# Moving the statistics sums of a convolution branch out of the accumulators' PSUM, with one-bank tiles at the seam between two layers

## The chip, the core and the metric

The kernel runs on one core of a Trainium2 chip, as one program. Its time is the device time of one execution in microseconds (us). The engines are PE (TensorE, matrix products, with PEld for its weight loads), DVE (VectorE), ACT (ScalarE), POOL (GpSimd) and SP (SyncE, which here only issues DMAs). Each engine runs its own list of instructions in order and waits on semaphores for the others.

## The reference

One inference step of a trunk of two layers on 640 tokens (128 of a prompt, 512 of a sample), width 1024, all in float32:

```python
# layer 0, the convolution branch (h: the normalised and modulated input)
u = h @ w_in + b_in                        # 1024 -> 3 x 2048
a, a_gate, z = split(u, 3)
v = a * sigmoid(a_gate)
v = depthwise_conv(v, w_dw, b_dw)          # 31 taps; the sample's in rows of 64 tokens
v = silu(layer_norm(v, ln_g, ln_b))        # over the 2048 channels
x = x + gate * ((v * silu(z)) @ w_out)     # 2048 -> 1024
# layer 1, a bidirectional state-space branch on modulate(rms_norm(x))
z, xbc, dt = split(h @ w_in, ...)
xbc = silu(depthwise_conv(xbc, 5 taps))
y = ssd_scan(forward) + flip(ssd_scan(backward)) + d * xs
x = x + gate * (rms_norm_by_group(y * silu(z)) @ w_out)
return rms_norm(x)                         # and the prompt's final states
```

The layer norm needs, for each token, the sum of v and of v squared over the 2048 channels. These are the statistics sums of this document.

## The kernel before

**Tiling.** Channels lie on the 128 partitions, tokens on the free axis: an activation is a tile of 128 x 640, used as two halves of 320. Each float32 product is three products in a faster format: a weight is split into a high part `wh` and a low part `wl`, an input into `h_hi` and `h_lo`, and PE adds `h_hi·wh`, `h_lo·wh` and `h_hi·wl`. Layer 0 has 48 tiles of `w_in` (16 each of a, g, the gate, and z); one is 48 matmuls of 128x320 (L499) into a PSUM tile `u` of two banks out of a ring of two (`mm`), with tokens in columns 0 to 319 of each bank; columns 480 on are used for blocks of the modulation (L519, L128).

**Weights.** SP loads `wf`, ACT casts it to `wh` (L472). `wl` is made in one of two ways in `split`: DVE or POOL subtracts `wh` from `wf` (L477), or ACT writes −`wh` (L482) and a DMA issued by POOL adds the weight from memory onto it (L483). The first tile of layer 0 and those of layer 1 take the first way, all others the second.

**Convolution.** v = a·sigmoid(g) is written on DVE (L539). For each of 16 tiles ACT starts an accumulator in PSUM (L640), DVE adds its taps there (L648), ACT forms some taps (`tp`, L678) that POOL adds into an SBUF tile `cv` (L719), POOL also does the edges of the prompt (`seam`, L703, L707), and at the end both are summed: by ACT's copy (L655) and POOL's adds, for the last two tiles by DVE (L668). Two PSUM tiles of 128 x 1024, `cva`, are the accumulators of the even and of the odd tiles (columns 0 to 639); their columns 640 to 799 hold the statistics sums, `ssum`. ACT squares `cv`, and PE adds `cv` and its square there with a matrix of ones, 8 matmuls of 160 columns for a tile, recorded as 16 (L195, `quarter_sums`), accumulating over all 16 tiles. So a sum and the taps of the next tiles write the same PSUM tile, and PE and DVE take turns there. After the sixteenth sum come mean and variance (L727 to L737), the normalisation, the product with silu(z), and the product with `w_out`: `out_pass` for the output tiles 0 to 5, `out_halves` for 6 and 7, which are done by halves of tokens (L853).

**Seam.** Here layer 0's last output tiles, the root mean square for layer 1 (`root`: sums L899, its reciprocal, and its spread over the partitions L919), the modulation (`modo`, L936, then `h_hi` on ACT and `h_lo`, L945, on DVE) and the first three tiles of layer 1 (`dt` and two `xs`, L874) follow each other. The output tiles are `o__5673` (6) and `o__5675` (7), two banks each, a half in each bank; the spread is written into `o__5673` too, and the `dt` product into `o__5675`.

**Order.** What each engine does when is decided while the program is built. Pieces of work are generators ("chains") that yield operations, keys they need and ring slots they take; a planner, `Order`, puts the operations of all chains in a row on each engine by estimated times and by priorities (`PRIO0`, and `PRIO` in layer 1), and that order is kept. The order of PE's tiles is written out (`PLAN0` and `PLAN`); `NPOOL` says how many taps of each convolution tile go to POOL.

Of the kernel before, what the change touches and what calls it, by code (L numbers as in the profile page):

```python
# [40 lines left out]
PRIO0 = {"conv": 1, "after_a": -2, "after_g": 2, "init": -6, "late_taps": 3, "late_adds": -4, "seam": 6, "copied": 2, "after_z": -6, "weights": 3, "split": -2, "row": -6, "square": -2, "filler": 6, "blocks": 7, "add_sums": 1, "stats": 3, "means": -6, "normalise": -1, "gate_z": -1, "late_block": 4, "residual": 6, "half_residual": -2, "root": 3, "modulation": 1, "split_h": 0, "scales": 6}  # L41
PLAN0 = "a1 g2 g3 a2 g4 a3 g5 a4 g6 a5 a6 g7 g8 z0 a7 a8 g9 g10 a9 a10 g11 g12 a11 z1 a12 g13 a13 z2 z3 z4 g14 g15 a14 z5 a15 z6 z7 z8 z9 z10 z11 z12 z13 z14 z15"
NPOOL = (11, 8, 15, 11, 6, 10, 12, 5, 3, 9, 2, 2, 5, 8, 7, 6)
# [4 lines left out]
def trunk(ctx: ExitStack, tc: tile.TileContext, a: dict):  # L48
# [308 lines left out]
    pa_ctx = ExitStack()  # L357
# [55 lines left out]
    with tc.tile_pool(name="l0", bufs=1) as lp:  # L413
# [4 lines left out]
        mr = lp.tile([P, 2, QN], F32, name="mr")  # L418
# [16 lines left out]
        for name, n in (("wf", 2), ("wh", 1), ("wl", 1), ("mm", 0), ("tm", 2), ("v", 4), ("cv0", 1), ("cv1", 1), ("cva", 0), ("cs", 33), ("tp", 3), ("pr", 1), ("eb", 3), ("hT", 0)):  # L435
            run.ring(name, n, 1.0 if name == "cs" else -9.0)
# [19 lines left out]
        def split(name, wf, src):  # L456
# [12 lines left out]
            else:  # L469
# [6 lines left out]
                if name[0] == "l1" or name == ("w", tiles0[0]):  # L476
                    t = yield either((VL, 1.23, lambda: V.tensor_sub(out=wl, in0=wf, in1=wh.bitcast(F32))), (PO, 2.44, lambda: G.tensor_sub(out=wl, in0=wf, in1=wh.bitcast(F32))), bias=0.0)  # L477
                    put("wf", t)
                    post(name, t)
                    return  # L480
# [53 lines left out]
        def after_a(i, ps, n=None):  # L534
# [15 lines left out]
        def after_z(j, ps, n=None):  # L550
# [4 lines left out]
            if n is not None:  # L555
                yield from late_block(n, ps)
                t = max(t, run.keys["mod", n])
            put("mm", t)
# [16 lines left out]
        def square(j):  # L575
            yield key(("cv", j))
            yield get("tm")
# [4 lines left out]
            start(add_sums(j), t)  # L582

        begun = []

        def add_sums(j):
            def sums():
                begun.append(j)
                for t_, s in ((cv[j], 0), (sgs["sq", j], 1)):
                    quarter_sums(ssum[s], t_, len(begun) == 1, len(begun) == 16)  # L590
            t = yield op(PE, 0.78, sums)
            put("tm", t)
            post(("sums", j), t)

        def filler():
            for name in plan:
# [13 lines left out]
                elif name[0] == "z":  # L610
                    start(after_z(i, ps, n), t)
                else:
# [3 lines left out]
                    start(after_a(i, ps, n), t)  # L616
# [9 lines left out]
        accs, whole = {}, []  # L626
# [8 lines left out]
        def init():  # L635
            for i in range(16):
                yield key(("v", i))
                yield get(f"cv{i % 2}")
                accs[i] = whole[i % 2][:, 0:NT]
# [12 lines left out]
        def copied(i):  # L652
# [3 lines left out]
            put(f"cv{i % 2}", t)  # L656
# [9 lines left out]
        def last_add(i):  # L666
            yield key(("added", i))
            t = yield op(VE, 0.9, lambda: V.tensor_add(out=cv[i], in0=cv[i], in1=accs[i]))  # L668
            post(("cv", i), t)
# [53 lines left out]
        def stats():  # L723
            t = yield key(*[("sums", j) for j in range(16)])
            rq = mr[:, 1]
            start(means(), t)
            yield op(ACT, 0.35, lambda: S.activation(out=msq, in_=ssum[0], func=AF.Square, scale=1.0 / 2048))  # L727
            yield op(VE, 0.37, lambda: V.scalar_tensor_tensor(out=rq, in0=ssum[1], scalar=1.0 / 2048, in1=msq, op0=ALU.mult, op1=ALU.subtract))
            post(("read",), run.clock[VE])
# [6 lines left out]
        def means():  # L736
            t = yield op(VE, 0.33, lambda: V.tensor_scalar(out=mr[:, 0], in0=ssum[0], scalar1=1.0 / 2048, scalar2=None, op0=ALU.mult))  # L737
            t = max(t, (yield key(("read",))))
            put("cva", t)
            put("cva", t)  # L740
            yield from spread_row(0, mr[:, 0])
# [75 lines left out]
        def residual(m, ps, ring):  # L817
# [4 lines left out]
            put(ring, t)  # L822
            yield get("tm")
# [10 lines left out]
        def out_halves():  # L834
            po = []
            for m, ring in ((6, "cva"), (7, "mm")):
                yield get(ring)
                po.append(bank(ring, f"o{m}_"))
            last["o"] = po
            start(spare(), 0.0)  # L840
            for b, tok in enumerate((slice(0, HN), slice(HN, NT))):
                ks = [k for it in ((0, 1, 2, 3) if b == 0 else (0, 2, 3, 1)) for k in range(4 * it, 4 * it + 4)]
                every = [(j, k) for k in ks[:12] for j in range(2)] + [(j, k) for j in range(2) for k in ks[12:]]
                for j, k in every:
                    if b == 0:
                        yield key(("out", 2, k // 4))
                    w = W0["out", 2, k // 4]

                    def step():
                        o = (k % 4 * 2 + j) * 128  # L850
                        wh, wl = (w[0][:, o : o + 128], w[1][:, o : o + 128]) if len(w) == 2 else (w[n + o // 512][:, o % 512 : o % 512 + 128] for n in (0, 2))
                        for n, (w_, t_) in enumerate(((wh, yh[k]), (wl, yh[k]), (wh, yl[k]))):
                            T.matmul(po[j][:, b, 0:HN], lhsT=w_, rhs=t_[:, tok], start=k == ks[0] and n == 0, stop=k == ks[-1] and n == 2)  # L853
# [6 lines left out]
            first[:] = [last["o"][1], last["mm"], last["cva"]]  # L860
            for b, tok in enumerate((slice(0, HN), slice(HN, NT))):
                for k in range(KD):
                    yield key(("h", b, k))
                    for n in range(3):
                        if not k and not b:
                            yield key(("l1", n))
                        if not k and not n:
                            yield key(("half", b, 7), ("o",))
                        ps, (wh, wl), (hi, lo) = first[n], W0["l1", n], h1[k]

                        def step():
                            ws, wls = wh[:, k * 128 : k * 128 + 128], wl[:, k * 128 : k * 128 + 128]
                            for n_, (w, t_) in enumerate(((ws, hi), (ws, lo), (wls, hi))):
                                T.matmul(ps[:, b, 0:HN], lhsT=w, rhs=t_[:, tok], start=k == 0 and n_ == 0, stop=k == KD - 1 and n_ == 2)  # L874
# [4 lines left out]
        last = {}  # L879

        def spare():
            for ring in ("mm", "cva"):
                yield get(ring)
                last[ring] = bank(ring, "xs")
            post(("o",), 0.0)

        def half_residual(b, m, ps, tok):
            for cd, sl in SEGS:
                xv = x[m][:, tok][:, sl]
                t = yield op(VE, 0.26 + 0.2 * cd, lambda: V.scalar_tensor_tensor(out=xv, in0=ps[:, b, sl], scalar=gain(0, m, cd), in1=xv, op0=ALU.mult, op1=ALU.add))  # L890
            post(("half", b, m), t)
            yield get("tp")
            sq = last["sq", b, m] = lp.tile([P, 560], F32, tag="tp", bufs=3, name="rms_sq")
# [3 lines left out]
        def sums_x(b, n, t, tok):  # L897
            for q in (2 * b, 2 * b + 1):
                T.matmul(last["mm"][32 * q : 32 * q + 32, b, HN : HN + QN], lhsT=ones[:, 0:32], rhs=t[:, tok][:, q % 2 * QN : q % 2 * QN + QN], start=n == 0, stop=n == 2)  # L899

        def root(b):
            tok = slice(b * HN, b * HN + HN)
            rows = slice(64 * b, 64 * b + 64)
            yield key(("acc", 5), ("o",))
            t = yield op(PE, 0.2, lambda: sums_x(b, 0, racc[0], tok))
            if b:
                put("tm", t)
            for n in range(2):
                yield key(("half_sq", b, 6 + n))
                t = yield op(PE, 0.2, lambda: sums_x(b, 1 + n, last["sq", b, 6 + n], slice(0, HN)))  # L910
                put("tp", t)
            rq = mr[:, 0][rows]
            ps = last["o"][0]
            yield op(ACT, 0.42, lambda: S.activation(out=rq, in_=last["mm"][rows, b, HN : HN + QN], func=AF.Sqrt, scale=1.0 / 1024, bias=epsb[rows]), "sqrt")
# [1033 lines left out]
```

## Time and profile before

| | |
|---|---|
| time, median of 3 runs | 1105.62 us (1105.17 to 1105.71) |
| profiled execution | 1108.58 us, span of its instructions 1106.8 us |
| mean granted clock of PE | 0.988 |
| PE busy | 1061.7 us (96%) |
| DVE busy | 804.6 us (73%) |
| ACT busy | 650.8 us (59%) |
| POOL busy | 448.5 us (41%) |
| taps on DVE (L648) | 360, 277.7 us, mean 822 ns |
| statistics sums on PE (L195) | 256 records of matmuls, from 116.0 to 385 us |

The profile is one execution, recorded by the hardware; its times are us from the first instruction, and busy time is time in which an engine executes. The granted clock is the share of full speed at which PE was allowed to run. Layer 0 takes the span up to about 575 us, its convolution up to 385; layer 1 the rest. Lines such as L648 are lines of the kernel before; in the kernel after the same statements have other numbers (the taps are L686, the products L501).

### The profile page before, as it was taken

Reading aid. Unit: us, or ns where it says so; the run is one execution under the profiler, and the core shown is the slowest. Engines: PE = TensorE matmul, PEld = TensorE weight load, DVE = VectorE, ACT = ScalarE, POOL = GpSimd, SP = SyncE. Lnnn points to the kernel's source line nnn. Section 1 sums busy time; section 2 is a strip of 40 time slices with the busy share of each in tenths; the row PEclk is TensorE's granted clock in tenths of the full one; section 3 lists DMA queues with packets and bytes.
Section 4 is the critical chain, followed back from the end, with each engine's and each line's share of the span. In section 5 each row is a group of like instructions: output and inputs, shape, how many; then the busy total and the mean of one; then the engine's idle time right before and its main releaser. Section 6 shows DMA issues by size and latency. Waiting matters only on the chain. (4 is left out here: it accounts for less than half of the span.)

```text
span 1106.8 us, 19938 instructions
## 1 busy us (share of the span) xinstructions
PE 1061.7 (96%) x7904; PEld 979.2 (88%) x7904; DVE 804.6 (73%) x1181; ACT 650.8 (59%) x1070; POOL 448.5 (41%) x447
## 2 busy tenths in 40 slices
PE   6989999999999999999999999999999999999996
PEld 4879999989999999999799888898899888988886
DVE  2588898999997889102479778987776786687763
ACT  6556887866558678333367564793537563754442
POOL 2027999866349601111000056405551534362223
PEclk9989999999999999999899999999999999999998
DMA  9398777886866667667112463414343423433102
GB/s 364 150 260 216 177 186 161 202 198 147 207 139 136 145 135 152 149 149 163 58 40 77 117 146 105 115 57 110 95 109 90 124 86 87 134 86 105 40 20 95
DMA packets 86685, 147.46 MB, mean 133 GB/s; under 512 B 26944, under 2 KB 49856, under 8 KB 86592
## 3 DMA queue, kind: packets, MB, share of 16 engines
q1 hardware_dynamic: 77088, 113.91, 34.6%
q0 software_dynamic: 8784, 31.46, 17.0%
q8 instruction: 62, 1.02, 0.4%
q10 hardware_dynamic: 720, 0.82, 0.2%
q14 instruction: 31, 0.25, 0.1%
HBM read 141.25 MB, written 4.92 MB: 132 GB/s over the span
## 5 line engine op out<-in xcount | busy, mean ns | idle before, releaser
L648 DVE SCALAR_TENSOR_TENSOR cva<-v,cst,cva 128x610 f32<-128x610 f32 (+13 forms) x360 | 277.7, 822 | 26.3 <-PE cva L195 13.3
L719 POOL TENSOR_TENSOR cv<-cv,tp 128x490 f32<-128x490 f32 (+6 forms) x120 | 151.6, 1264 | 8.2
L472 ACT CAST wh<-wf 128x1024 fp32r<-128x1024 f32 x63 | 65.8, 1044 | 91.0 <-PE o__5231 L153 29.8
L1071 ACT CAST wh<-wf 128x1024 fp32r<-128x1024 f32 x53 | 55.5, 1048 | 87.1 <-PE o L1109 32.7
L678 ACT ACTIVATE tp<-v,cst 128x490 f32<-128x490 f32 (+6 forms) x120 | 83.0, 722 | 32.7 <-POOL cv L719 32.1
L1109 PE MATMUL o<-yhl,wh 128*128 128x320 f32 x384 | 94.0, 332 | 2.0 <-ACT zs L1228 1.9
L1075 DVE TENSOR_TENSOR wl<-wf,wh 128x1024 fp32r<-128x1024 f32 x49 | 65.0, 1326 | 31.0 <-ACT wh L1071 30.8
L1109 PE MATMUL pz<-h_hi,wh 128*128 128x320 f32 x256 | 85.5, 334 | 1.5 <-ACT up L1138 1.5
L1395 POOL TENSOR_TENSOR y<-y,yo 128x512 f32<-128x512 f32 x32 | 48.5, 1517 | 79.5 <-DVE yo L1393 79.5
L1109 PE MATMUL pz<-h_hi,wl 128*128 128x320 f32 x256 | 79.1, 309 | 0.0
L1109 PE MATMUL pz<-h_lo,wh 128*128 128x320 f32 x256 | 79.0, 309 | 0.0
L483 POOL DMA_DIRECT2D wl<-w_in x44 | 38.5, 874 | 97.2 <-ACT wl L482 89.8
L1109 PE MATMUL xs<-h_hi,wh 128*128 128x320 f32 x224 | 77.2, 344 | 0.0
L1109 PEld LDWEIGHTS o<-yhl,wh 128*128 128x128 f32 x384 | 64.6, 190 | 11.3 <-issue 8.5
L1151 DVE SCALAR_TENSOR_TENSOR xs<-up,cst,xs 128x642 f32<-128x642 f32 x64 | 69.1, 1081 | 2.0 <-ACT xs L1149 0.6
L1109 PE MATMUL xs<-h_hi,wl 128*128 128x320 f32 x224 | 69.2, 309 | 0.0
L1109 PE MATMUL xs<-h_lo,wh 128*128 128x320 f32 x224 | 69.1, 309 | 0.0
L482 ACT ACTIVATE wl<-wh 128x1024 fp32r<-128x1024 f32 x59 | 62.6, 1060 | 1.7
L1270 ACT ACTIVATE gf<-gf,cols 128x128 f32<-128x128 f32 x160 | 50.3, 393 | 20.8 <-DVE gf L1266 20.6
L1109 PE MATMUL o<-yhl,wl 128*128 128x320 f32 x192 | 59.7, 311 | 0.0
L1264 POOL TENSOR_TENSOR gb<-gb,cols 128x512 f32<-128x512 f32 x20 | 27.3, 1367 | 68.7 <-DMA gb<-acd 68.7
L1109 PEld LDWEIGHTS pz<-h_hi,wh 128*128 128x128 f32 x256 | 48.2, 188 | 5.1 <-issue 3.4
(753 smaller groups left out, 3413.8 us busy)
## 6 DMA issues: line engine op xcount, KB each, us to landing
wf<-w_in SPq DMA_DIRECT2D x48, 512.0 KB, 3.8
wl<-w_in POOLq DMA_DIRECT2D x44, 512.0 KB, 6.8
wa<-w_ada SPq DMA_DIRECT2D x64, 256.0 KB, 6.3
wf<-w_out SPq DMA_DIRECT2D x32, 512.0 KB, 3.7
wf<-w_xbc SPq DMA_DIRECT2D x24, 512.0 KB, 3.7
gf<-acd SPq DMA_DIRECT2D x40, 256.0 KB, 5.0
wa<-w_ada SPq DMA_DIRECT2D x16, 512.0 KB, 10.2
wf<-w_z SPq DMA_DIRECT2D x16, 512.0 KB, 4.1
```

The source lines that it names most:

```text
L472: t = yield op(ACT, 1.05, lambda: S.copy(out=wh, in_=wf))
L482: yield op(ACT, 1.06, lambda: S.activation(out=wl, in_=wh.bitcast(F32), func=AF.Copy, scale=-1.0))
L483: t = yield op(PD, 0.7, lambda: G.dma_start(out=wl, in_=src, accum_op=ALU.add))
L648: t = yield op(VE, 0.24 + 0.01 * (hi - lo), lambda: V.scalar_tensor_tensor(out=rows64(accs[i], lo, hi), in0=rows64(vs[i], lo + d, hi + d), ...
L678: t = yield op(ACT, 0.72, lambda: S.activation(out=tp[:, :, 0 : hi - lo], in_=rows64(vs[i], lo + d, hi + d), func=AF.Copy, scale=w_dw(i, t ...
L719: t = yield op(PO, 1.28 + 0.0175 * (hi - lo - 49), lambda: G.tensor_add(out=rows64(cv[i], lo, hi), in0=rows64(cv[i], lo, hi), in1=sgs["tp" ...
L1071: S.copy(out=cell["wh"], in_=cell["wf"])
L1075: e_.tensor_sub(out=cell["wl"], in0=cell["wf"], in1=cell["wh"].bitcast(F32))
L1109: T.matmul(ps[:, b, at_ : at_ + t1 - t0], lhsT=w_, rhs=t_[:, t0:t1], start=k == 0 and n == 0, stop=k == nk - 1 and n == 2)
L1151: t = yield op(VL, 0.89, lambda: V.scalar_tensor_tensor(out=acc, in0=u[:, d : d + PW], scalar=c("w_c", j * 5 + d), in1=acc, op0=ALU.mult, ...
L1270: t = yield op(ACT, 0.39, lambda: S.activation(out=gv[:, h_, :], in_=gv[:, h_, :], func=AF.Exp, bias=cols1[ch][:, o8 + h_ : o8 + h_ + 1]), ...
L1395: t = yield op(PO, 1.29, lambda: G.tensor_add(out=y, in0=y, in1=yo))
```

## The change

1. **Sums.** The sums of a tile go into the PSUM tile of an `a` or `z` product, behind its last matmul: `cv` into columns 320 to 479 of its first bank, the square into those of its second (`side_sums`). Then DVE adds both (128 x 2 x 160) to an SBUF tile `ssum` (`add_sums`, L612: one copy and 13 adds), before the product's PSUM tile is given back. The last two tiles' sums go into a `cva` tile of their own (`late_sums`), and one more DVE add joins them. The accumulators are now a plain ring of two PSUM tiles, given back after their last read.
2. **Weights.** The second tile of layer 0 also gets its `wl` by subtraction.
3. **Seam.** After the residuals of the output tiles 2 and 3 the accumulators' pool is closed and a pool of four one-bank tiles (`hb`) opened. The halves of the output tiles 6 and 7, the second root, and the halves of the third tile of layer 1 each get such a tile; the first root gets an `mm` tile. The spread root is copied to an SBUF tile `rs` by ACT (L977), and the modulation (L994) reads that.
4. **Tables.** `PRIO0`, `PLAN0` and `NPOOL` are new (119 taps on POOL in place of 120, so 361 on DVE); layer 1 gets `PRIO1` and `PLAN1`, another order of its tiles.

The diff, cut:

```diff
-PLAN0 = "a1 g2 g3 a2 g4 a3 g5 a4 g6 a5 a6 g7 g8 z0 a7 a8 g9 g10 ...
-NPOOL = (11, 8, 15, 11, 6, 10, 12, 5, 3, 9, 2, 2, 5, 8, 7, 6)
+PLAN0 = "a1 g2 a2 g3 a3 z0 z1 g4 a4 g5 a5 g6 a6 g7 z2 a7 g8 a8 ...
+NPOOL = (10, 5, 12, 7, 10, 3, 10, 6, 9, 12, 10, 2, 11, 4, 2, 6)
...
-                if name[0] == "l1" or name == ("w", tiles0[0]):
+                if name[0] == "l1" or name in (("w", tiles0[0]), ("w", tiles0[1])):
...
-        def after_a(i, ps, n=None):
+        def after_a(i, ps, n=None, j=None):
...
+            if j is not None:
+                t = yield from add_sums(j, ps)
             put("mm", t)
...
-        def add_sums(j):
-            def sums():
-                begun.append(j)
-                for t_, s in ((cv[j], 0), (sgs["sq", j], 1)):
-                    quarter_sums(ssum[s], t_, len(begun) == 1, len(begun) == 16)
-            t = yield op(PE, 0.78, sums)
+        def side_sums(ps, t):
+            js = [j for j in ready if ready[j] <= t + 0.2]
+            if late or not js:
+                return None, t
+            j = min(js)
+            ...
+            t = yield op(PE, 0.78, lambda: sums_of(j, ps[:, 0, HN : HN + QN], ps[:, 1, HN : HN + QN], True, True))
+            put("tm", t)
+            put("sq", t)
+            return j, t
+
+        def add_sums(j, ps):
+            n = len(summed)
+            summed.append(j)
+            t = yield op(VE, 0.49, lambda: V.tensor_add(out=ssum, in0=ssum, in1=ps[:, :, HN : HN + QN]) if n else V.tensor_copy(out=ssum, in_=ps[:, :, HN : HN + QN]))
+            post(("summed", j), t)
+            return t
+
+        def late_sums():
+            yield key(("cv", 14))
+            yield get("cva")
+            pst = cvp.tile([P, 1024], F32, tag="cva", bufs=2, name="pst").rearrange("p (a n) -> p a n", a=2)
+            ...
...
+        pools["h"] = h_ctx.enter_context(tc.tile_pool(name="hps", bufs=1, space=PSUM))
+            for _ in range(4):
+                put("hb", 0.0)
...
-            start(modulation(b, ps, tok), t)
+            yield op(PE, 0.66, spread_rq)
+            ...
+            t = yield op(ACT, 0.47, lambda: S.copy(out=rs, in_=out))
+            put("hb" if b else "mm", t)
+            start(modulation(b, rs, tok), t)
...
-        PLAN = "z00 x02 c0 b0 x03 c1 x10 z01 z02 x20 x11 x12 x21 z03 ...
+PLAN1 = "z00 x21 x03 b0 c0 x02 z01 x13 b1 x10 x11 z02 x12 z03 x20 ...
```

**Where instructions move.** First place, the start of layer 0 on POOL: its first DMAs for low weights (L483, after L485; a row "x3" stands for three) and the prompt's edges of the first convolution tile (`seam`). Before:

```order
L425 MEMSET eb_642 128x60
L483 DMA wl<-w_in 128x1024
L703 TENSOR_TENSOR seam<-eb_638,cst_92 128x450
L707 TENSOR_TENSOR seam<-seam 128x2x105
L707 TENSOR_TENSOR seam<-seam 128x2x60
L707 TENSOR_TENSOR seam<-seam 128x2x30
L707 TENSOR_TENSOR seam<-seam 128x2x15
L483 DMA wl<-w_in 128x1024 x3
```

After:

```order
L427 MEMSET eb_642 128x60
L742 TENSOR_TENSOR seam<-eb_638,cst_92 128x450
L746 TENSOR_TENSOR seam<-seam 128x2x105
L746 TENSOR_TENSOR seam<-seam 128x2x60
L746 TENSOR_TENSOR seam<-seam 128x2x30
L746 TENSOR_TENSOR seam<-seam 128x2x15
L485 DMA wl<-w_in 128x1024 x4
```

The DMA for the second tile is gone from the head; the first one is now that of the third tile, behind the edges as before.

Second place, PE at the first convolution tile's sums. Before (the product's tile is `u__1248`):

```order
L499 MATMUL u__1248<-h_lo,wh 128x320
L499 MATMUL u__1248<-h_hi,wl 128x320
L195 MATMUL cva<-cv_943,ones 32x160 x4
L195 MATMUL cva<-sq,ones 32x160 x4
L499 MATMUL u__1248<-h_hi,wh 128x320
L499 MATMUL u__1248<-h_lo,wh 128x320
```

After:

```order
L501 MATMUL u__1132<-h_lo,wh 128x320
L501 MATMUL u__1132<-h_hi,wl 128x320
L197 MATMUL u__1132<-cv_965,ones 32x160 x4
L197 MATMUL u__1132<-sq,ones 32x160 x4
L501 MATMUL u__1223<-h_hi,wh 128x320
L501 MATMUL u__1223<-h_lo,wh 128x320
```

The sums stood in the middle of a product and wrote `cva`; they now stand between two products and write the PSUM tile of the one just done.

Third place, DVE at the seam, the first half of tokens. Before:

```order
L936 SCALAR_TENSOR_TENSOR modo<-x_70,gsc_85,o__5673 128x64
L945 SCALAR_TENSOR_TENSOR h_lo<-modo,mod_83,h_hi 128x64
L936 SCALAR_TENSOR_TENSOR modo<-x_70,gsc_85,o__5673 128x256
L945 SCALAR_TENSOR_TENSOR h_lo<-modo,mod_83,h_hi 128x256
L945 SCALAR_TENSOR_TENSOR h_lo<-modo,mod_83,h_hi 128x64
L936 SCALAR_TENSOR_TENSOR modo<-x_71,gsc_85,o__5673 128x64
```

After:

```order
L479 TENSOR_TENSOR wl<-wf,wh 128x1024 x2
L994 SCALAR_TENSOR_TENSOR modo<-x_67,gsc_85,rs 128x64
L994 SCALAR_TENSOR_TENSOR modo<-x_67,gsc_85,rs 128x256
L994 SCALAR_TENSOR_TENSOR modo<-x_68,gsc_85,rs 128x64
L994 SCALAR_TENSOR_TENSOR modo<-x_68,gsc_85,rs 128x256
L994 SCALAR_TENSOR_TENSOR modo<-x_69,gsc_85,rs 128x64
L994 SCALAR_TENSOR_TENSOR modo<-x_69,gsc_85,rs 128x256
L1002 SCALAR_TENSOR_TENSOR h_lo<-modo,mod_83,h_hi 128x64
```

The modulation reads `rs` in SBUF in place of the output tile's PSUM, and two weight splits of layer 1 stand ahead of its first instruction.

More of the change, by code (lines that the diff above doesn't have):

```diff
@@ L736, in means @@
         def means():
[L737 to L741, printed above, removed]
+            yield key(("squared",))
+            t = yield op(VE, 0.33, lambda: V.tensor_scalar(out=ssum[:, 0], in0=ssum[:, 0], scalar1=1.0 / 2048, scalar2=None, op0=ALU.mult))
+            yield from spread_row(0, ssum[:, 0])
         pmr = [None, None]
@@ L877, in out_halves, with half_bank @@
                             run.ends.append(t)
[L879 to L885, printed above, removed]
+            first[:] = [ps[0][1], ps[1][1], (ps[2][1], ps[3][1])]
+        pools = {}
+        def half_bank(name):
+            return pools["h"].tile([P, 512], F32, tag="hb", bufs=4, name=name)
         def half_residual(b, m, ps, tok):
@@ L976, in trunk @@
             cvp = pa_ctx.enter_context(tc.tile_pool(name="cvps", bufs=1, space=PSUM))
-            whole += [cvp.tile([P, 1024], F32, tag="cva", bufs=2, name="cva") for _ in range(2)]
-            ssum = [z_[:, NT : NT + QN] for z_ in whole]
             start(after_a(0, first[1][1]), -0.9)
@@ L987, in trunk @@
             start(stats(), 0.0)
+            start(late_sums(), 0.0)
             start(normalise(), 0.0)
@@ L1664, in item @@
             items.append((gen, src))
-        PLAN = "z00 x02 c0 b0 x03 c1 x10 z01 z02 x20 x11 x12 x21 z03 x13 b1 x30 c2 z10 x22 o00 x31 z11 o01 o02 o03 b2 x23 z12 b3 z13 x32 x33 z20 z21 o10 o11 c3 z22 z23 z30 z31 o12 o13 z32 o20 z33 o21 o22 o23"
-        for name in PLAN.split():
+        for name in PLAN1.split():
             g, *j = (int(d) for d in name[1:])
```

147 lines of the change are left out of this document (92 added, 55 removed).

## The prediction

> **What bounds the kernel now.** I read the page first (busy shares), then the waits of TensorE, then a table of stretches, then the timeline at the long waits.
>
> ```profile
> span 1106.8 us, 19938 instructions
> PE 1061.7 (96%) x7904; PEld 979.2 (88%) x7904; DVE 804.6 (73%) x1181; ACT 650.8 (59%) x1070; POOL 448.5 (41%) x447
> ```
>
> PE is busy for 1061.7 of 1106.8 us; PE is the bound, and a change pays only where it shortens PE's 45 us of idle time or the short stretches in which its granted clock is below full. PE's instructions are the same in kind and number after the change. The waits of PE that the change touches:
>
> ```profile
> PE u__765 L499 <- DMA wl<-w_in: 4.3, 1, 4.3
> PE cva L195 <- DVE cva L648: 3.0, 6, 1.0
> PE o__5673 L853 <- DVE modo L936: 2.1, 5, 0.6
> PE o L1109 <- ACT zs L1228: 1.9, 1, 1.9
> PE cva L195 <- POOL seam L707: 1.6, 3, 0.6
> ...
> PE cva L195 <- ACT tp L678: 1.3, 1, 1.3
> PE cva L195 <- POOL cv L719: 1.3, 1, 1.3
> ```
>
> (In total us, times, longest.) Where they lie, by stretches; the columns are PE, PEld, DVE, ACT, POOL busy, then the granted clock, the DMA share and GB/s:
>
> ```profile
> 50.00:75.00 25.00, 20.36 (x146) 19.44 (x145) 16.45 (x23) 14.31 (x22) 5.66 (x11) 0.88 0.69 199
> 56.00:382.70 326.70, 314.57 (x2658) 300.85 (x2657) 291.65 (x394) 228.04 (x334) 228.40 (x261) 0.99 0.76 182
> 375.00:525.00 150.00, 149.98 (x1038) 148.82 (x1037) 67.02 (x94) 81.50 (x95) 19.87 (x23) 1.00 0.70 150
> 525.00:550.00 25.00, 22.88 (x128) 19.98 (x127) 11.51 (x25) 9.41 (x16) 0.00 (x0) 0.87 0.13 43
> 575.00:750.00 175.00, 171.50 (x1179) 158.05 (x1180) 149.86 (x197) 119.24 (x218) 50.64 (x37) 1.00 0.41 107
> 750.00:775.00 25.00, 23.09 (x151) 20.29 (x151) 19.12 (x28) 7.66 (x12) 14.40 (x10) 0.93 0.45 101
> 775.00:1075.00 300.00, 295.99 (x2001) 259.91 (x2000) 220.66 (x330) 152.42 (x291) 119.03 (x91) 1.00 0.33 90
> ```
>
> So PE loses time at four places: the second weight tile (50 to 75), the sixteen statistics sums in the convolution stage (the rest of the 326.70 − 314.57 = 12.1 us), the seam (525 to 550), and a scatter in layer 1. From 375 to 525 it loses nothing.
>
> **Start: the weight split of the second tile (g2).** PE waits, and then runs at half rate:
>
> ```profile
> 69.84 0.64 PE L499 MATMUL u__765<-h_hi,wl 128*128 128x320 f32 x1 [4.34 <-DMA wl<-w_in]
> 70.27 0.47 PE L499 MATMUL u__765<-h_hi,wh 128*128 128x320 f32 x1
> ...
> 75.87 0.39 PE L499 MATMUL u__765<-h_hi,wh 128*128 128x320 f32 x1
> 76.10 0.30 PE L499 MATMUL u__765<-h_lo,wh 128*128 128x320 f32 x1
> ...
> 76.97 0.31 PE L499 MATMUL u__765<-h_lo,wh 128*128 128x320 f32 x1
> ```
>
> From 70.27 to 75.87 stand 21 steps of 0.267 us, from 76.10 to 76.97 six of 0.145. So the stall is 4.34 us, and the slow stretch costs (76.1 − 69.8) × (1 − 0.145/0.267) = 2.9 us; the clock of the first row of stretches, 25 × (1 − 0.88) = 3.0 us, agrees. Together 7.3 us. PE wanted the low half at 69.84 − 4.34 = 65.5. After the change DVE subtracts it (1.22 us by the L477 row below) where before POOL issued a transfer with 9.0 us of way (next rows): it is ready about 61, and this wait goes. What is late next is the third tile, now a2, whose low half still goes the slow way, and whose rows of before are these:
>
> ```profile
> 64.49 1.05 ACT L472 CAST wh<-wf 128x1024 fp32r<-128x1024 f32 x1 [2.31 <-DMA wf<-w_in]
> 66.93 0.88 POOL L483 DMA_DIRECT2D wl<-w_in  x1 [1.69 <-ACT wl L482]
> wl<-w_in POOLq DMA_DIRECT2D x3, 512.0 KB, 9.0
> ```
>
> PE comes to a2's first low half one tile after 65.5, a tile being 48 × 0.145 = 7.0 us: at 72.5. Issued at 66.93 and 9.0 us under way, it would land at 75.9: a stall of 3.4 us. But its load (on which the cast waited 2.31 us) no longer shares the queues with g2's accumulating transfer; I take 1.4 us off for that, an estimate between nothing and the 3.4 that would hide it all, so a stall of 2.0. A slow stretch would follow if it acts as the 1.91 us wait of layer 1 did, whose 25 us show 0.93, or 1.75 us lost. New cost 3.8, between 0 and 3.4 + 3.0 = 6.4. Net for the start: −3.5 (−7.3 to −0.9).
>
> The page "TensorE: Matmul & The Clock Gate" of the Trainium skill (Part 1, The HAM clock gate) says that the half rate comes only after a whole idle window of about 3.4 us. Here the trace disagrees: the wait of 1.91 us, and at the seam five waits of 2.1 us together, came with a stretch at a lower clock. By the page's rule a stall of 2.0 us would cost no clock, and the start and the whole would give 1.8 us more; the trace decides, and I keep the 1.75.
>
> **Convolution: the sums leave the accumulators' tiles.** In before, taps on DVE and sums on PE take turns in the same two PSUM tiles, and each blocks the other:
>
> ```profile
>   PE cva L195: 13.3, 15
>   ACT cva L640: 8.6, 4
> ...
> L477 DVE TENSOR_TENSOR wl<-wf,wh 128x1024 fp32r<-128x1024 f32 x4 | 4.9, 1222 | 0.6 <-ACT wh L472 0.6
> L1535 DVE SCALAR_TENSOR_TENSOR zs<-zs,cst,rms 128x320 f32<-128x320 f32 x32 | 15.6, 540 | 1.6 <-PE rms L1525 1.5
> 381.70 0.82 DVE L668 TENSOR_TENSOR cv<-cv,cva 128x640 f32<-128x640 f32 x1
> 384.79 0.48 PE L195 MATMUL cva<-cv,ones 128*32 128x160 f32 x8
> ```
>
> (The first two lines: idle time in us of DVE before its taps, times, and the releaser.) PE's side is 3.0 + 1.6 + 1.3 + 1.3 = 7.2 us. After the change a sum stands behind a tile's last product, in that tile's own PSUM, and waits only for cv (POOL) and its square (ACT); both were done early enough in before for the gaps not to exceed 1.3 us while the wait for DVE came on top. I take all 7.2 off, between nothing (the waits change their name) and 7.2.
>
> DVE pays: 14 instructions on 128x320 at 0.54 (the L1535 row) = 7.6, one more add at the end 0.54, one tap more (361 for 360) 0.82, as the add at 381.70, and the split of g2, 1.22: +10.1 us. It gets back the 13.3 us in which it waited for PE's sums. Do the adds hurt? PE comes to the sixteenth tile's sum at 384.8 − 3.5 − 7.2 = 374.1. DVE's last add of before ended at 382.5, so DVE must end 8.4 us earlier although it has more to do. If DVE keeps all its other idle time (326.7 − 291.7 = 35.0, less 13.3) it ends at 382.5 + 10.1 − 13.3 = 379.3, 5 us late; if the 8.6 us also go in which it waited for the first value of a tile, which ACT could not write until the accumulator was free of its sum, it ends at 370.7, 3.4 us early; with no idle at all at 357.8. I take 370.7: the accumulator now comes free with its own last read. So DVE's cost is covered by PE's products; if the cover fails, the price is a rival's below. Behind the add on DVE stand the taps of the next tiles, and the mm tile stays held until it is done: PE needs it back one whole tile (7 us) later, which is long beside 0.54. ACT and POOL carry on with their work beside it (228 of 327 us busy each).
>
> The page "PSUM — Partial Sum Buffer" (PSUM bank collisions raise a hardware error) of the Trainium skill asks that engines be kept apart by bank, not by address; the 13.3 us above are what that costs here, and the change puts the sums into banks which ACT and DVE read, too. That gives a rival of its own, below.
>
> **Seam.** In before the spread of the root (L919) and the last two output tiles share PSUM, so that PE's products wait for DVE's reads:
>
> ```profile
> 536.19 0.81 PE L919 MATMUL o__5673<-mr,cst 64*128 64x160 f32 x4
> 540.01 0.28 DVE L936 SCALAR_TENSOR_TENSOR modo<-x,gsc,o__5673 128x64 f32<-128x64 f32 x1 [0.54 <-PE o__5673 L853]
> 540.21 0.28 DVE L945 SCALAR_TENSOR_TENSOR h_lo<-modo,mod,h_hi 128x64 fp32r<-128x64 f32 x1
> 540.41 0.47 DVE L936 SCALAR_TENSOR_TENSOR modo<-x,gsc,o__5673 128x256 f32<-128x256 f32 x1
> 540.80 0.48 DVE L945 SCALAR_TENSOR_TENSOR h_lo<-modo,mod,h_hi 128x256 fp32r<-128x256 f32 x1
> 550.05 0.47 PE L874 MATMUL o__5675<-h_hi,wh 128*128 128x320 f32 x1
> ```
>
> The waits are 2.1 us and the clock of 525 to 550 loses 25 × (1 − 0.87) = 3.25 us: 5.4 in all. After it ACT copies the root to SBUF (0.47, the price of the 256-wide row) and DVE reads that; the products go through. What is late next: PE then needs layer 1's first input 48 products (7.0 us) after the spread where it took 13.9, and after that one of sixteen inputs every 9 × 0.145 = 1.3 us; DVE needs about 1.2 us for each (starts 0.20 and 0.39 apart, twice), and three weight splits of 1.22, which stand between. PE's last need is 7.0 + 15 × 1.3 = 26.5 us after the spread; DVE's sum is 0.5 + 16 × 1.2 + 3.7 + four residual adds 1.5 + 1.2 for the second root = 26.1. It is even, so I put 1.2 us of small waits back (0 to 5.4). Net −4.2.
>
> **Layer 1's new order.** It moves tiles, and adds no work on PE. What there is to win is PE's idle time: 3.5 + 1.9 + 4.0 us in the three stretches after 575, and 1.75 of clock, 11.2 in all, each with another cause. The trace does not show the new order; bounds are all of the 1.9 + 1.75 stall and as much again of the scatter gained, or a like amount lost: ±5. I take 0.
>
> **Sum.** −3.5 − 7.2 − 4.2 + 0 = −14.9 us. The profiled execution took 1108.58 us, its span 1106.8; 1108.6 − 14.9 = 1093.7. The median of the runs is 1105.62, 3 us below the profiled one, and 1105.6 − 14.9 = 1090.7: I forecast 1091.
>
> **The rivals.**
> - *DVE becomes the bound at the last sum (slower).* For it: DVE is busy 291.7 of 326.7 us in this stage and gets 10.1 more. If all its idle time stays, it ends at 382.5 + 10.1 = 392.6, and PE, at 374.1, waits 18.5 us and pays about 3 of clock: 1091 + 21 = 1112. It is slower than before once DVE ends later than 374.1 + 14.9 − 3 = 386. Against it: 13.3 of its idle time has its cause in the tiles that are no longer shared. 0.06.
> - *DVE is a little late.* With 379.3 PE waits 5 us, and 3 of clock: 1091 + 8 = 1099. The accumulators' first writes, 8.6 us, would have to stay. 0.12.
> - *The banks still collide.* The new sums go into banks from which ACT and DVE take the tile's products, and DVE's add waits for PE's sum, 14 times at the 0.9 us of before (13.3/15): 12.4 us of DVE's idle time stay, DVE ends at 370.7 + 12.4 = 383.1, PE waits 9.0 and pays 3: 1103, about no change. Against it: the sum ends 0.78 us after the last product, while DVE has taps of other tiles to do. It is what the Trainium skill's page on PSUM would lead one to expect. 0.05.
> - *The waits only change their names.* Sums wait for POOL and ACT as before, up to 7.2: 1098. 0.07.
> - *Layer 1 decides.* Its order is worse by 5 or better by 5: 1096 or 1086. 0.12 each way.
> - *My forecast*, 1087 to 1095, 0.46.
>
> **How the numbers follow.** A change under 0.2%, or 2.2 us, is about what a measurement of this kernel can't tell from none. Above 1107.8 lie most of the first rival, and a case in which several stages give nothing: 0.07. Within 1103.4 to 1107.8 lies half of the bank rival and the tails of the others: 0.05. Faster has the rest, 0.88. The range takes in the start's full gain and a better layer 1 (1091 − 4 − 5 = 1082) below, and the late DVE at 1099 with a little more of a stall at the third tile (+3) above: 1082 to 1102.
>
> **What the profile after would show.** Right: no wait of the g2 tile for wl, a wait of 0 to 3.6 us at the third tile near 72; sums waiting under 1 us in all, DVE's last add near 371 and PE's last sum without a gap; no wait of L897 at the seam and a clock near 1.00 there. Wrong: the sums' waits by other names, a gap of PE before the sixteenth sum, PE waiting for h in the first products of layer 1 by more than a few us, or new waits past 575 that sum to more than 11.2 us.

## The result, and the profile after

| | before | after |
|---|---|---|
| time, median of 4 runs | 1105.66 us (1105.17 to 1105.82) | 1088.06 us (1086.83 to 1089.37) |
| profiled execution, span | 1106.8 us | 1087.5 us |
| mean granted clock | 0.988 | 0.988 |
| PE busy | 1061.7 us | 1052.7 us |
| DVE busy | 804.6 us | 808.6 us |

The ratio is 0.9842 (0.9825 to 0.9859): 17.6 us less, where 14.9 were forecast. The waits of PE after, in the same view as before (total us, times, longest):

```profile
PE pt L1821 <- DVE v L1757: 3.7, 1, 3.7
PE u__858 L501 <- DMA wl<-w_in: 2.0, 1, 2.0
PE o__4974 L155 <- ACT sz L557: 1.9, 1, 1.9
PE pz L1164 <- ACT up L1195: 1.4, 1, 1.4
PE po L1446 <- DVE stn L1411: 1.3, 2, 1.0
...
PE dt L922 <- DVE h_lo L1002: 0.2, 1, 0.2
```

No wait for `cva` and none for `modo` is left. Two of the long ones are new: at the third tile's low weight half (`u__858`), and at the second output tile (`o__4974`), six matmuls into the output pass. That of `pt` in layer 1 is an old one that has grown; in before it read:

```profile
PE pt L1765 <- DVE v L1701: 1.5, 1, 1.5
```

The stretches of after (PE, PEld, DVE, ACT, POOL busy, granted clock, DMA share, GB/s); the kernel after is up to 20 us further on with its work than before at the same time:

```profile
50.00:75.00 25.00, 22.66 (x178) 21.74 (x177) 18.20 (x25) 15.69 (x24) 5.59 (x11) 1.00 0.65 194
75.00:100.00 25.00, 25.00 (x185) 24.78 (x186) 23.43 (x34) 13.20 (x21) 14.34 (x14) 0.93 0.86 227
100.00:375.00 275.00, 275.00 (x2408) 268.44 (x2407) 262.15 (x362) 207.79 (x302) 207.45 (x237) 1.00 0.76 181
375.00:525.00 150.00, 148.11 (x1002) 146.16 (x1001) 62.25 (x87) 79.51 (x92) 17.32 (x20) 0.99 0.62 137
525.00:550.00 25.00, 24.80 (x169) 23.69 (x168) 22.79 (x69) 14.63 (x38) 0.00 (x0) 1.00 0.14 45
575.00:750.00 175.00, 169.72 (x1149) 155.16 (x1149) 142.26 (x189) 115.66 (x211) 54.75 (x43) 0.98 0.39 102
750.00:775.00 25.00, 23.95 (x153) 20.58 (x152) 20.95 (x26) 15.66 (x31) 13.12 (x11) 1.00 0.43 106
775.00:1075.00 300.00, 298.52 (x2044) 265.39 (x2043) 210.90 (x337) 153.00 (x281) 113.95 (x91) 1.00 0.32 85
```

From 100 to 375 PE has not one idle instant, through all the sums. The seam (525 to 550) is nearly full and at full clock. Against that stand the slow stretch after the third tile's wait (0.93), the loss from 375 to 525, which was none before, and a lower clock from 575 to 750.

Between the first and the last product of each kind in the two traces the time went like this: first to last `w_in` product 406.3 to 390.0 us (start and sums, −16.2), from there to the first `pz` product of layer 1 147.2 to 144.1 (outputs and seam, −3.1), to the last product with `yhl` 516.4 to 515.1 (layer 1, −1.3), the rest (ahead of the first and behind the last) +1.4. The −3.1 holds two things that go against each other: the new wait of 1.9 us at `o__4974` and the slow stretch behind it lie in it, 3.4 us together, and the seam itself gains more.

That DVE had the time for its adds is read at the end of the convolution, on its timeline and on PE's (start, duration):

```profile
366.36 0.82 DVE L706 TENSOR_TENSOR cv<-cv,cva 128x640 f32<-128x640 f32 x1
369.77 0.49 DVE L765 TENSOR_TENSOR ssum<-ssum,pst 128x320 f32<-128x320 f32 x1 [2.59 <-PE pst L197]
```

```profile
368.95 0.48 PE L197 MATMUL pst<-cv,ones 128*32 128x160 f32 x8
```

What DVE still waits for ahead of its taps (idle us, times):

```profile
  ACT cva L678: 3.7, 3
```

DVE's last add ends at 367.2, 1.8 us ahead of PE's last sum. The 13.3 us in which taps waited for sums are gone, and 4.9 of the 8.6 in which they waited for ACT's first value.

### The profile page after: what moved, and what is told of

The parts are those of the page before. It is cut to its first block, busy times and chain, and to the rows that moved or that the text cites. A ratio compares the mean times of both kernels' runs of the same rounds, so it can differ in the third digit from the quotient of the medians.

```text
span 1087.5 us, 19939 instructions
## 1 busy us (share of the span) xinstructions
PE 1052.7 (97%) x7904; PEld 979.9 (90%) x7904; DVE 808.6 (74%) x1195; ACT 665.0 (61%) x1085; POOL 439.9 (40%) x446
## 5 line engine op out<-in xcount | busy, mean ns | idle before, releaser
L686 DVE SCALAR_TENSOR_TENSOR cva<-v,cst,cva 128x600 f32<-128x600 f32 (+13 forms) x361 | 279.7, 822 | 8.6 <-ACT cva L678 3.7
L758 POOL TENSOR_TENSOR cv<-cv,tp 128x490 f32<-128x490 f32 (+5 forms) x119 | 151.5, 1273 | 7.8
L717 ACT ACTIVATE tp<-v,cst 128x490 f32<-128x490 f32 (+5 forms) x119 | 82.2, 720 | 24.9 <-POOL cv L758 24.4
L1130 DVE TENSOR_TENSOR wl<-wf,wh 128x1024 fp32r<-128x1024 f32 x48 | 67.3, 1402 | 31.4 <-ACT wh L1126 31.1
L1164 PE MATMUL pz<-h_hi,wh 128*128 128x320 f32 x256 | 88.3, 345 | 1.4 <-ACT up L1195 1.4
L1452 POOL TENSOR_TENSOR y<-y,yo 128x512 f32<-128x512 f32 x32 | 45.3, 1417 | 87.1 <-DVE yo L1450 83.8
L1208 DVE SCALAR_TENSOR_TENSOR xs<-up,cst,xs 128x642 f32<-128x642 f32 x64 | 65.9, 1030 | 7.4 <-PE ptx L1232 3.4
L485 POOL DMA_DIRECT2D wl<-w_in x43 | 37.5, 872 | 71.1 <-ACT wl L484 58.4
L1164 PEld LDWEIGHTS pz<-h_lo,wh 128*128 128x128 f32 x256 | 48.2, 188 | 3.8 <-issue 3.8
```

The lines of the kernel that those rows point to most:

```text
L485: t = yield op(PD, 0.7, lambda: G.dma_start(out=wl, in_=src, accum_op=ALU.add))
L686: t = yield op(VE, 0.24 + 0.01 * (hi - lo), lambda: V.scalar_tensor_tensor(out=rows64(accs[i], lo, hi), in0=rows64(vs[i], lo + d, hi + d), ...
L717: t = yield op(ACT, 0.72, lambda: S.activation(out=tp[:, :, 0 : hi - lo], in_=rows64(vs[i], lo + d, hi + d), func=AF.Copy, scale=w_dw(i, t ...
L758: t = yield op(PO, 1.28 + 0.0175 * (hi - lo - 49), lambda: G.tensor_add(out=rows64(cv[i], lo, hi), in0=rows64(cv[i], lo, hi), in1=sgs["tp" ...
L1130: e_.tensor_sub(out=cell["wl"], in0=cell["wf"], in1=cell["wh"].bitcast(F32))
L1164: T.matmul(ps[:, b, at_ : at_ + t1 - t0], lhsT=w_, rhs=t_[:, t0:t1], start=k == 0 and n == 0, stop=k == nk - 1 and n == 2)
```

## The experiments

Each kernel ran beside the kernel before on one chip, and its ratio to before is compared with that of after, which was measured twice (0.9842, and 0.9855 beside e10 to e12). "Against after" is the difference to their mean, 0.9848, times 1105.66 us; the intervals of the ratios make that uncertain by 2 to 3 us.

| kernel | ratio to before, 95% | against after |
|---|---|---|
| e1, layer 1's tables of before | 0.9879 (0.9856 to 0.9902) | +3.4 us |
| e2, g2 by transfer again | 0.9866 (0.9848 to 0.9885) | +2.0 |
| e3, third tile by subtraction too | 0.9835 (0.9815 to 0.9855) | −1.4 |
| e4, sums back in the accumulators | 0.9934 (0.9918 to 0.9950) | +9.5 |
| e5, seam of before | 0.9874 (0.9853 to 0.9895) | +2.9 |
| e6, no copy of the root | 0.9876 (0.9863 to 0.9888) | +3.1 |
| e7, silu(z) earlier on ACT | 0.9807 (0.9792 to 0.9823) | −4.5 |
| e8, time steps earlier on DVE | 0.9816 (0.9801 to 0.9831) | −3.5 |
| e9, after again | 0.9855 (0.9828 to 0.9883) | |
| e10, e7 and e8 together | 0.9795 (0.9769 to 0.9820) | −5.9 |
| e11, e10 and e3 together | 0.9793 (0.9764 to 0.9821) | −6.1 |
| e12, before with g2 by subtraction | 0.9950 (0.9934 to 0.9966) | |

**e4, the sums.** `ssum` is again columns 640 to 799 of two accumulator tiles held throughout, and the sums are a chain of their own:

```diff
-                    j, t = yield from side_sums(ps, t)
-                    start(after_a(i, ps, n, j), t)
+                    start(after_a(i, ps, n), t)
...
+            whole += [cvp.tile([P, 1024], F32, tag="cva", bufs=2, name="cva") for _ in range(2)]
+            ssum = [z_[:, NT : NT + QN] for z_ in whole]
```

> The kernel after, with the statistics sums back in columns 640 to 799 of two fixed accumulator tiles, as a chain of their own in the middle of products; weights, seam and tables as after (the planner orders anew). Theory: sharing the PSUM tiles costs PE what the traces say, 16 sums at 23.8 us from the product before to the one after, against 12.9: +10.9 us, 1099; the shown waits come back (about 7 us) and some 3 us more which no wait shows. Theory of the forecast: +7.2, 1095. Rival: the gain came from the new tables and not from the place of the sums: 1091 or less.

It is +9.5 us. Its waits of PE:

```profile
PE cva L197 <- DVE cva L656: 6.2, 9, 1.5
...
PE cva L197 <- ACT cv L663: 0.5, 1, 0.5
PE cva L197 <- DVE mod L137: 0.4, 1, 0.4
```

The tables of after are kept here, and the waits are back, most of them for the taps on DVE. (e4 moves the sums in PSUM and in PE's order at once; the two are not tried apart.) Counted from the start of the instruction ahead of a sum to the start of the one behind it, the 16 sums take 23.8 us in before, 23.4 in e4 and 12.9 in after, while the idle time shown ahead of them is 7.5, 7.4 and 0. By this count the sums' new place is worth 10.5 to 10.9 us, and 3 us of that no wait shows. About half of these 3 us are inside the waits: a sum between two products without a wait costs 0.92 us, one with a wait of w costs about 0.1 more than 0.92 + w. The rest is that most sums of after stand beside the small matmuls of the modulation, where one costs 0.75 to 0.86 by this count: that part belongs to their place in the order.

**e2, e3 and e12, the start.** In e2 the second tile's condition is taken back, in e3 it is widened to the third tile, and e12 is the kernel before with the condition of after:

```diff
e2
-                if name[0] == "l1" or name in (("w", tiles0[0]), ("w", tiles0[1])):
+                if name[0] == "l1" or name == ("w", tiles0[0]):
e3
+                if name[0] == "l1" or name in (("w", tiles0[0]), ("w", tiles0[1]), ("w", tiles0[2])):
e12
-                if name[0] == "l1" or name == ("w", tiles0[0]):
+                if name[0] == "l1" or name in (("w", tiles0[0]), ("w", tiles0[1])):
```

> The kernel after, with the low half of the second tile (g2) made by the accumulating transfer again. Theory: the 4.3 us wait and its slow stretch (2.9 us) come back at 70 us, the 2.0 us wait of the third tile with its stretch (1.75) goes: 7.2 - 3.8 = +3.4 us, 1091.5. Rival 1: only the wait's place moves, since each tile's transfer is late by about as much: 1088. Rival 2: the third tile waits too, behind g2's transfer on the queue: +7, 1095.

> The kernel after, with the low half of the third tile (a2) made by subtraction too. Theory: its wait of 2.0 us and the slow stretch behind it (25 us at 0.93, 1.75 us) go, the fourth tile has 7 us more for its transfer and is in time: -3.8 us, 1084. DVE has 1.2 us more to do, covered. Rival: the fourth tile (g3) takes over the wait, because its load also comes later: 1087 to 1089.

> The kernel before, with the low half of its second tile by subtraction and nothing else (the planner orders anew). Theory: the 4.3 us wait and the stretch behind it go, the third tile waits 2 to 3.4 us in its stead: -3.5 us (-1 to -5), 0.9968 of before. Rival: its third tile, whose transfer came 6 us after g2's, is in time and all 7.2 us come: 0.9935.

The waits of PE in e2 and then in e3:

```profile
PE u__764 L501 <- DMA wl<-w_in: 4.0, 1, 4.0
```

```profile
PE u__1126 L197 <- ACT sq L586: 0.9, 1, 0.9
PE u__1126 L197 <- POOL cv L758: 0.8, 1, 0.8
```

e2 has the second tile's wait back and none at the third: +2.0 us, between the theory (+3.4) and nothing, and not the +7. In e3 the third tile's wait is gone and the fourth has none, but now PE is at the first sum 1.7 us before POOL and ACT: most of the 2.0 us is only moved, −1.4 in place of the −3.8 expected. Neither theory had named this wait. In e12 the third tile waits 0.85 us, and its ratio is 0.9950, −5.5 us, with an interval of −3.8 to −7.3: between the theory's −3.5 and the rival's −7.2, and both are at its edge. Not all of it is the start's: the planner's new order also shortened the 16 sums there, from 23.8 to 22.3 us. So the start is worth 2 to 5.5 us by e2 and e12; what fixes it more closely stays open.

**e5 and e6, the seam.** e5 has before's `out_halves`, `half_residual`, `root` and `modulation` in place of after's. e6 leaves out the copy to SBUF:

```diff
-            rs = tmp.tile([P, NT], F32, tag="tm", bufs=2, name="rs")[:, 0:HN] if b else ...
-            t = yield op(ACT, 0.47, lambda: S.copy(out=rs, in_=out))
-            put("hb" if b else "mm", t)
-            start(modulation(b, rs, tok), t)
+            start(modulation(b, out, tok, "hb" if b else "mm"), run.clock[PE])
```

> The kernel after, with the seam as before: output tiles 6 and 7 in two-bank tiles, the root's spread in tile 6's PSUM, the modulation reading it there, the third tile of layer 1 in a two-bank tile; sums, weights and tables as after (the planner orders anew). Theory: the seam gave the 7 us by which the excess of PE's starts fell there between the two traces: 1095; the waits for modo come back. Forecast's theory: 4.2 us, 1092. Rival: the new tables alone would have spread the seam's waits, the tiles do nothing: 1089 or less.

> The kernel after, without ACT's copy of the spread root: the modulation on DVE reads the spread in its own PSUM tile (one bank of its own, or an mm tile), which is held until then. Theory: what counts is that no product of PE writes a bank that DVE reads, not where DVE reads from; no wait for modo comes back, 1088 within 1.5 (the copy of 0.47 falls out of the chain, the tile is held longer). Rival: reading the spread from PSUM is what blocked PE: the waits of 2 us and a slow stretch return, 1091 or more.

The waits of PE at the seam in e5, and then in e6:

```profile
PE o__5700 L894 <- DVE modo L977: 2.1, 5, 0.6
```

```profile
PE rms L973 <- DVE msq L969: 1.8, 1, 1.8
...
PE rms L959 <- ACT rms_sq L941: 1.3, 2, 0.7
...
PE xs L922 <- DVE modo L990: 0.7, 1, 0.7
```

e5 brings back the same five waits of 2.1 us, with the new tables, and is +2.9 us: what removes these waits is the seam's code, and not the tables. e6 came out as neither theory said. No output product waits for `modo`, as the first theory had it, yet it is +3.1 us. Without the copy the root's PSUM tile is held until DVE has read it for all eight channel tiles; `xs` waits for that (0.7), and the second root stands earlier in PE's order, where its squares and its reciprocal are not ready (1.3 and 1.8, with a stretch at half clock from 532.2 us on). So both parts of the seam's change are needed here: with banks of their own no output product waits for `modo`, and without the copy the time is lost again. How much of that is the bank held longer, and how much the other order of the second root, is not tried apart.

**e1 and e8, layer 1.** e1 has before's `PRIO` and `PLAN`. e8 changes one priority:

```diff
-PRIO1 = {..., "time_steps": 2, ...}
+PRIO1 = {..., "time_steps": -8, ...}
```

> The kernel after, with layer 1's two tables of before. Theory: layer 1's new order gave little, 1.3 us by the two traces (516.4 to 515.1 us from the first pz product to the last output product), because the 1.9 and 1.5 us waits that it removes come back as one of 3.7 (pt waits for v). Then the time is 1089 to 1091, and the 3.7 us wait is gone from the trace. Rival: layer 1's order carries what the forecast had too small, 3 us or more: 1091.5 or higher.

> The kernel after, with the chain of the time steps in layer 1 given priority on DVE over the convolutions there (the planner orders layer 1 anew). Theory: the wait of 3.7 us (pt for v) comes from taps and a weight split that DVE does ahead of it; with its slow stretch it is worth 5.2 us: 1083. Rival: DVE is full there, the taps that are late instead hold PE as long: 1087 to 1089.

e1 is +3.4 us, which its interval can't tell from the 1.3 of the traces nor from 5; it leans to the rival. In its profile the wait of `pt` for `v` is down to 1.0 us, and waits of 2.4 (`o` for `zs`), 1.6 and 1.5 us stand at other places. What the 3.7 us wait of after consists of is seen on DVE's timeline there; PE waits until 598.7:

```profile
592.11 3.64 DVE L1208 SCALAR_TENSOR_TENSOR B<-up,cst,B 128x642 f32<-128x642 f32 x4
595.67 1.22 DVE L1130 TENSOR_TENSOR wl<-wf,wh 128x1024 fp32r<-128x1024 f32 x1
596.92 0.56 DVE L1757 TENSOR_TENSOR t<-rp 64x384 f32<-64x384 f32 x1
597.51 0.56 DVE L1754 SCALAR_TENSOR_TENSOR v<-xr,v 128x384 f32<-128x384 f32 x1
598.10 0.56 DVE L1757 TENSOR_TENSOR v<-v,rp 128x384 f32<-128x384 f32 x1
```

Four taps and a weight split, 4.8 us, stand ahead of the last three steps to `v`. With the steps first the wait is gone, and the weight split is what comes late instead:

```profile
PE xs L1164 <- DVE wl L1130: 2.4, 1, 2.4
```

The gain is 3.5 us by the medians, between the 5.2 and the 1 of the two expectations; the profiled executions, 1088.43 and 1089.37, differ by 0.9.

**e7, the output pass.** One priority:

```diff
-PRIO0 = {..., "after_z": -5, ...}
+PRIO0 = {..., "after_z": -6, ...}
```

> The kernel after, with one priority changed so that ACT, at the end of a z tile, writes silu(z) ahead of the cast and the negative copy of the next weight, as before did (the orders of the other engines stay nearly the same). Theory: the new wait of 1.9 us at the first output product is that order, since the silu frees the PSUM tile 2.1 us too late; it goes, and with it the slow stretch that followed it in some executions (1.6 us): 1085 to 1086.5. Rival: something else holds the output product at that place, or the weight comes 0.8 us late in its stead: 1087.5 to 1088.5.

ACT at the last z tile, in before, in after and then in e7:

```profile
428.41 0.80 ACT L553 ACTIVATE sz<-u__4852,cst 128x640 f32<-128x640 f32 x1 [1.05 <-PE u__4852 L499]
429.11 1.04 ACT L472 CAST wh<-wf 128x1024 fp32r<-128x1024 f32 x1
```

```profile
412.43 1.05 ACT L474 CAST wh<-wf 128x1024 fp32r<-128x1024 f32 x1 [0.34 <-PE u__4878 L501]
413.51 1.06 ACT L484 ACTIVATE wl<-wh 128x1024 fp32r<-128x1024 f32 x1
414.47 0.78 ACT L557 ACTIVATE sz<-u__4878,cst 128x640 f32<-128x640 f32 x1
```

```profile
413.92 1.05 ACT L474 CAST wh<-wf 128x1024 fp32r<-128x1024 f32 x1 [0.19 <-PE u__4878 L501]
414.87 0.79 ACT L557 ACTIVATE sz<-u__4878,cst 128x640 f32<-128x640 f32 x1
415.56 1.05 ACT L484 ACTIVATE wl<-wh 128x1024 fp32r<-128x1024 f32 x1
```

And the wait of PE that is left in e7:

```profile
PE o__4970 L155 <- ACT sz L557: 0.8, 1, 0.8
```

The z product's PSUM tile is freed by `sz`, and the second output tile takes it over (the expectation calls this place the first output product). In before `sz` came first; in after two weight steps of 2.1 us stand ahead of it, in e7 one, and the wait falls from 1.9 to 0.8. The time falls by 4.5 us, more than the wait and its stretch can give (1.1 + 1.5); the uncertainty of 2 us and the stretches at other places, which this edit does not control, may hold the rest, but that is not shown.

**e9, e10 and e11.**

> The kernel after, unchanged, beside the next three on one chip. Theory: its time varies by 2 to 3 us from one execution to the next with the slow stretches that follow its waits of 1.9 to 3.7 us (75, 415 and 599 us) in some of them and not in others: a lower mean granted clock goes with a longer time, the waits themselves stay the same within 0.5 us, and the ratio to before stays within 0.982 to 0.986. Rival: the waits themselves vary.

> The kernel after, with silu(z) ahead of the weight work on ACT and the time steps ahead of the convolutions on DVE together. Theory: the two gains are at two places and add up: 0.9842 - 0.0035 - 0.0026 = 0.978 of before, 1081.5. Rival: no more than the better of the two, 0.981.

> As the kernel before this one, and the third tile's low half by subtraction too. Theory: the wait of 2 us at 75 us goes, but the first sum at 105 us waits 1.7 us for POOL and ACT in its stead, as it did with this edit alone: 0 to -1.5 us beside it. Rival: with silu(z) earlier on ACT the square is in time as well: -3.5 us.

In e9 the waits are 1.76, 1.90 and 3.66 us where the first profile of after has 2.04, 1.89 and 3.66; the one at 75 us had no slow stretch this time, and the execution was 1.9 us shorter. Its other four executions were at a clock of 0.988 and 1089.7 to 1092.3 us long, the profiled one at 0.990 and 1087.4. That fits the theory, as far as two profiles go; only profiled executions show where their stretches lie. The clock does not order all times: of the first four executions of after, 1089.14 us had 0.990 and 1086.83 had 0.989, and one of e3 had 0.942 at 1091.42. And the rival has a part: in the eight other profiles with the weights made as in after (e1 and e4 to e10) the wait at the third tile is 0.9 to 3.1 us. e10 and e11 are the fastest kernels, 0.9795 and 0.9793 of before; on the same chip after had 1091.19 us and they 1083.73 and 1083.53. Against the mean of after the two gains together are −5.9 us where their own runs make −8.0; beside the after of the same chip they are −7.5. With e10's interval of ±2.8 us that can't tell a full sum from a part. The third one adds nothing that could be told (−0.2).

## Why the prediction was right, point by point

**Start, −3.5.** The second tile's wait went, and the third tile, forecast to wait 2.0 us from 72.5, waited 2.04 from 72.9. That the two agree so well is luck. The forecast took 1.4 us off because the tile's load would come sooner; it came later. The cast waited 3.73 us for it where it had waited 2.31, and the low half's transfer was issued 0.8 us later than forecast:

```profile
67.69 1.01 POOL L485 DMA_DIRECT2D wl<-w_in  x1 [5.00 <-ACT wl L484]
```

PE went on at 74.97, so the transfer took at most 7.3 us where the forecast had 9.0, and PE came to the tile 0.4 us later than forecast: +0.8, −1.7 and −0.4 happen to make the 1.4 that was taken off. The slow stretch behind the wait, put at 1.75, came in the profiled execution (0.93 in the stretch) and not in e9. e2 and e12 bound the term at 2 to 5.5 us.

**Sums, −7.2.** The mechanism was right and the size was not: 10.9 us by the traces, 9.5 by e4. The step that failed is the one that took PE's gain from the waits shown. "All 7.2 off" was the upper end of the range; a wait costs more than the idle time that is shown (1.6 us over the 16 sums), and the sums became cheaper by where they stand (1.8 us).

**DVE's cover.** Forecast: DVE ends at 370.7, 3.4 us before PE's last sum. Measured: 367.2, and 1.8 us. Each side ended earlier than forecast, DVE by 3.5 us and PE by about 5. Of the 8.6 us that the forecast took off for the first values, 3.7 stayed. An add took 0.49 us for 0.54. So the rival in which DVE becomes the bound stayed away by 1.8 us, no more. The bank rival, drawn from the Trainium skill's page "PSUM — Partial Sum Buffer" (PSUM bank collisions raise a hardware error), did not come: in the stretch from 100 to 375 PE has no idle time at all, and DVE shows none ahead of any of its fourteen adds (L612).

**Output pass, nothing.** Missed. The wait of 1.9 us at the second output tile, with a stretch in some executions, is new. The forecast held the stretch from 375 to 525 to be safe because PE was gapless there; the new priorities put ACT's weight steps ahead of the silu that frees PE's tile. e7 shows it.

**Seam, −4.2.** Right in its mechanism: the five waits went, and e5 brings them back for +2.9 us. The size is less sure. 3.25 us of the term were the slow stretch that before's profile shows at the seam, and neither e5 nor e12 has it there, with the same five waits. In the two traces the seam gives about 6.5 us (the −3.1 without the new wait and its stretch, 3.4), some 3 of them that stretch. The small waits put back at 1.2 us were 0.2.

**Layer 1, 0 ± 5.** −1.3 by the traces, −3.4 by e1; within the bounds. The waits of before for `zs` (1.9) and `ysq` (1.5) went, and the one for `v` grew from 1.5 to 3.7.

**Sum.** −14.9 forecast, −17.6 measured, and −16.0 when after was measured again. The sums' 2 to 4 us too little, and 1 to 3 in layer 1, outweigh the missed wait in the output pass (1.9 us, 3.4 with its stretch). That the total came so near is partly luck, since these misses have opposite signs.

## What to carry to other kernels

When two engines take turns in one PSUM tile, price it by the time from the start of the instruction ahead to the start of the one behind, not by the idle time shown: here 10.9 us for 7.5. After a new order, look first at who frees the bound engine's buffers and what stands ahead of that on its engine: one priority brought 4.5 us, no less than the seam's new tiles (2.9) as far as these runs can tell. A wait that is taken away at the head of a chain (e3) shows what is late next; take the one behind it into the same forecast.

## What the runs showed of the hardware

Whether a wait is followed by a slow stretch depends on its length and on how it falls in time. Over the 14 profiles, each of the 11 waits of PE of 3.1 us and more between 50 and 1050 us was followed by a stretch of matmuls at half rate; of the 23 waits of 1.75 to 2.6 us 14 were and 9 were not; of the waits of 1.3 to 1.64 us none was. The same wait of 1.9 us at the output pass had one in five profiles and none in four. At the five short waits of the seam (2.1 us together) before had one, e5 and e12 none.

The traces' record of the granted clock shows more. Every stretch between 50 and 1050 us lasts 3.41 us or twice that (why twice stays open), and within an execution the clock changes only on a grid of 3.41 us. Cut this time along the grid: each of the 24 windows at full clock in which PE is idle, as the trace draws it, for 55% or more is followed by a window at half clock; of the five idle for 50 to 54% one is; of all the others only one, at the seam of before (36%). A wait of 1.9 us is 55% of a window. In after it falls inside one (413.4 to 415.3 us in the window from 413.2 to 416.6), and a stretch follows; in e2 a border cuts it (418.2 to 420.1, border at 418.4), and none does. Where the grid lies differs between executions, of one kernel too (after and e9), so for such a wait the stretch is chance.

A stretch of 3.41 us, with matmuls every 0.267 us in place of 0.147, costs about 1.5 us. The Trainium skill's page "TensorE: Matmul & The Clock Gate" (Part 1, The HAM clock gate) says that the clock gate looks at a free-running window of 3.4 us; the grid agrees with that. Its rule that only gaps over about 3.4 us count (HAM oscillation) does not hold here: 14 of 23 gaps of up to 2.6 us were followed by a stretch. The executions of one kernel differ in their mean clock: e5 took 1089.98 to 1092.1 us at 0.991 to 0.992, and 1094.62 to 1096.79 at 0.987 to 0.989.
